# One transposing step and 512-column value products for each head of a differential attention

## The chip, the core and the metric

The kernel runs on one core of a Trainium2 chip. The metric is the time of one execution on the device in microseconds (us). Before the change it is 1768.67 us, the median of three runs (1768.25 to 1769.67). The engines are called PE (TensorE), DVE (VectorE), ACT (ScalarE), POOL (GpSimd) and SP (SyncE, which here issues most of the transfers).

## The reference, cut to what matters

The program is a trunk of two layers over 512 tokens of width 1024. Each layer computes three token mixers beside each other (a differential attention, a convolution module, a neighbourhood attention), merges them by gates, and adds a SwiGLU feed-forward part and a gated embedding. The change touches the differential attention alone. It has four heads in each layer, with two sets of queries and keys of width 64 and values of width 128:

```python
    def block(qi):
        s = jnp.einsum('bhcqd,bhckd->bhcqk', qi, k).astype(f32) * scale
        a = jax.nn.softmax(s, axis=-1)
        a = (a[:, :, 0] - lam * a[:, :, 1]).astype(v.dtype)
        return jnp.einsum('bhqk,bhkd->bhqd', a, v)

    o = lax.map(block, qb)
    o = o.transpose(1, 2, 0, 3, 4).reshape(B, HA, S, DV_A)
    o = rmsnorm(o, subln_g) * (1.0 - lam_init)
```

So for each head and each block of 128 queries there are two softmaxes over all 512 keys, their weighted difference, and the product with the values. The result is normalized over the value width.

## The kernel before

**Layout.** Activations lie with channels on the 128 partitions and the 512 tokens along the free axis. A matrix product of full precision is made of three products of a reduced format (`mm3`, lines 179 to 183): each operand is split in a high and a low part (`split`, lines 166 to 168: a copy on ACT gives the high part, a subtraction on DVE the low one), and high by high, high by low and low by high are accumulated. Weights are split the same way as they arrive (`weights`, lines 170 to 177, tiles named wr, wh and wl).

**Order of the work.** PE's instructions run in the order in which the program writes them. On the other engines a scheduler arranges the instructions when the kernel is built; in general the place in the program is the priority, and weight splits are put ahead. On the chip each engine then works through its list in order.

The long projections are written as loops of `mm3`. `chunk` (lines 119 to 122) counts these triples, and every fourth one is a tick (`tick`, lines 98 to 109), so a tick is 12 products of 512 columns. At each tick the small pieces of the attentions are put between the projection's products: first every running generator whose time has come makes its next step, then, where the gap since the last one has passed, the first unit in the queue is started. A `yield n` in such a generator means that it goes on n ticks later.

**A differential head.** `diff_in` (line 830) projects a head's queries and keys, applies the rotary embedding on DVE (tiles named rp; the halves are swapped by four transfers, line 846), splits the result and stacks high and low parts by transfers (`stack`, line 664). Then it queues four units, one for each block of 128 queries, at a gap of two ticks. Each unit calls `probs` (line 909): two score tiles of 128x512 in PSUM, four products; a maximum on DVE for each; two exponentials on ACT; and on DVE the difference of the two, which stays in a tile named a. The pool has three buffers of a, four of e (the second exponential) and two of b.

Every second unit goes on. Three ticks later it transposes the probabilities of its 256 queries on PE (line 876): eight transposes of 128x128 into two PSUM tiles (tag tr, two buffers), each of them for two of the four key blocks. Each PSUM tile is split into a tile pt of high and low parts. Two ticks later the products with the values follow: four key blocks, three products each, 256 columns wide, into one half of the accumulator av. After the second half the accumulator is squared and copied on ACT, and the norm over the value width runs with transposes one tick and three ticks later.

Between these pieces stand the projections of later heads, the value projections (`values`, products of 256 columns, line 619), and the gates (`gate_c`, `gate_b`). The taps of the convolution (tiles conv_z, line 164) are filled in on DVE as background work, behind chosen instructions.

Of the kernel before, what the change touches and what calls it, by code (L numbers as in the profile page):

```python
# [12 lines left out]
F32R = mybir.dt.float32r  # L13
# [7 lines left out]
P = 128  # L21
# [44 lines left out]
class Net:  # L66
# [794 lines left out]
    def diff_unit(self, head, qt, st4, k2, st, box, ys):  # L861

        nc, i = self.nc, self.i
        half, t = qt // 2, qt % 2
        box[qt] = self.probs(st4, k2, qt, box["s0"])
        if t == 0:
            return
        yield 3
        ats = [box[2 * half], box[2 * half + 1]]
        pps = []  # L870
        for kp in range(2):
            pt = self.ps("tr", (P, 2, 256))
            for u in range(2):
                for t in range(2):
                    kc = 2 * kp + u
                    nc.tensor.transpose(pt[:, u, t * P:(t + 1) * P],
                                        ats[t][:, kc * P:(kc + 1) * P], self.ident)
            pp = self.sb("pt", [P, 2, 2, 256], F32R)
            self.split(pp[:, 0], pp[:, 1], pt)
            pps.append(pp)  # L880
        yield 2
        if half == 0:
            box["av"] = self.ps("av")
        av = box["av"]
        cs = slice((head % 2) * P, (head % 2) * P + P)
        for kp in range(2):
            for u in range(2):
                v = st["v", head // 2][kp][:, u].rearrange("p (a b) -> p a b", a=2)
                self.mm3(av[:, half * 256:half * 256 + 256], v[:, 0, cs], v[:, 1, cs],
                         pps[kp][:, 0, u], pps[kp][:, 1, u], kp * 2 + u == 0, kp * 2 + u == 3)  # L890
        if half == 0:
            return

        eps = self.sb("sm", [P, 4])
        self.stt(eps, box["s0"], EPS, box["s0"], ALU.mult, ALU.mult)
        o = self.sb("t", [P, 512])
        sq = self.sb("ss", [P, 512])
        self.act(sq, av, AF.Square)
        self.act(o, av, AF.Copy, scale=self.subg[:, i:i + 1])

        def done(col, bc):
            self.tt(o, o, bc, ALU.mult)
            y = self.sb("y", [P, 2, 512], F32R)
            self.split(y[:, 0, :], y[:, 1, :], o)
            ys.append(y)

        yield from self.norm(sq, P, (1, 2), done, spread=False, eps=eps)

    def probs(self, st4, k2, qt, s0):


        nc, i = self.nc, self.i
        qs = slice(qt * P, (qt + 1) * P)
        m = self.sb("s", [P, 10])
        es = []
        for u in range(2):
            sc = self.ps("sc")
            self.scores(sc, st4, k2, u, qs, slice(0, 512))
            nc.vector.tensor_reduce(out=m[:, u:u + 1], in_=sc, op=ALU.max, axis=AX.X, negate=True)  # L919
            e = self.sb("e" if u else "a", [P, 512])  # L920
            self.act(e, sc, AF.Exp, table="exp", bias=m[:, u:u + 1],
                     accum_out=m[:, 3:4] if u else s0[:, qt:qt + 1])
            es.append(e)
        nc.vector.reciprocal(m[:, 4:5], m[:, 3:4])
        self.stt(m[:, 5:6], m[:, 4:5], self.nlam[:, i:i + 1], s0[:, qt:qt + 1],
                 ALU.mult, ALU.mult)
        self.stt(es[0], es[1], m[:, 5:6], es[0], ALU.mult, ALU.add)
        return es[0]
# [555 lines left out]
```

## Time and profile before

The profile is of one execution.

| what | before |
|---|---|
| median of the runs (lowest, highest) | 1768.67 us (1768.25, 1769.67) |
| span of the profiled execution | 1766.6 us |
| time from the span to the median | 2.1 us |
| PE busy | 1759.3 us, 100% |
| DVE busy | 1408.6 us, 80% |
| ACT busy | 885.5 us, 50% |
| POOL busy | 98.4 us, 6% |
| the chain that ended last | PE 92%, DVE 4%, DMA 2%, ACT 2% |

The span runs from the first to the last instruction of the program. The profiled execution's own time is its span and the little around it; the table sets the span beside the median of the runs. A row of the timeline has the start in us, the length in us, the engine, the line, the operation, the tile written and the tiles read, the shape, and how many such instructions follow each other; in brackets the idle time of the engine before it and what ended it. Matmuls overlap in PE's pipeline, so the length of one is more than the distance to the next.

### The profile page before, as it was taken

Reading aid. Unit: us, or ns where it says so; the run is one execution under the profiler, and the core shown is the slowest. Engines: PE = TensorE matmul, PEld = TensorE weight load, DVE = VectorE, ACT = ScalarE, POOL = GpSimd, SP = SyncE. Lnnn points to the kernel's source line nnn. Section 1 sums busy time; section 2 is a strip of 40 time slices with the busy share of each in tenths; the row PEclk is TensorE's granted clock in tenths of the full one; section 3 lists DMA queues with packets and bytes.
Section 4 is the critical chain, followed back from the end, with each engine's and each line's share of the span. In section 5 each row is a group of like instructions: output and inputs, shape, how many; then the busy total and the mean of one; then the engine's idle time right before and its main releaser. Section 6 shows DMA issues by size and latency. Waiting matters only on the chain.

```text
span 1766.6 us, 27127 instructions
## 1 busy us (share of the span) xinstructions
PE 1759.3 (100%) x10146; PEld 1551.8 (88%) x10146; DVE 1408.6 (80%) x2354; ACT 885.5 (50%) x1529; POOL 98.4 (6%) x114
## 2 busy tenths in 40 slices
PE   9999999999999999999999999999999999999998
PEld 7888888888899899998888888888888998989987
DVE  7967988998898587787777688889887976867776
ACT  5576555325565254454545655552356643534444
POOL 0000000000111010100000000000001110101000
PEclk9999999999999999999999999999999999999999
DMA  6575641334757365544446655322356674655332
GB/s 231 158 186 160 162 123 54 102 100 150 222 153 196 106 173 156 137 126 127 151 137 173 180 148 154 108 73 94 101 183 194 168 179 118 172 141 156 99 104 96
DMA packets 112548, 253.95 MB, mean 144 GB/s; under 512 B 14368, under 2 KB 23328, under 8 KB 112416
## 3 DMA queue, kind: packets, MB, share of 16 engines
q1 hardware_dynamic: 99024, 227.83, 42.0%
q0 software_dynamic: 12672, 23.07, 8.1%
q8 instruction: 80, 1.31, 0.3%
q10 hardware_dynamic: 720, 1.31, 0.2%
q14 instruction: 52, 0.43, 0.1%
HBM read 214.41 MB, written 7.34 MB: 126 GB/s over the span
## 4 chain that ended last, share of the span: by engine, by line
PE 92%; DVE 4%; DMA 2%; ACT 2%; issue 1%; SPq 0%; POOL 0%; ACTq 0%; POOLq 0%; DVEq 0%
PE ffn_mm L1034 4%; PE ffn_mm L1036 4%; PE ffn_mm L182 4%; PE ffn_mm L181 4%; PE ffn_mm L183 4%; PE ffn_mm L1035 4%; PE ffn_sc L1036 3%; PE ffn_sc L1034 3%; PE ffn_sc L1035 3%; PE mergea_mm L182 2%; PE mergea_mm L183 2%; PE mergea_mm L181 2%; PE gateb_mm L182 2%; PE gateb_mm L183 2%; PE gateb_mm L181 2%; PE wo_mm L182 2%
## 5 line engine op out<-in xcount | busy, mean ns | idle before, releaser
L164 DVE SCALAR_TENSOR_TENSOR conv_z<-glu_z,pre_par,conv_z 128x512 f32<-128x512 f32 x240 | 179.6, 748 | 3.5
L147 ACT ACTIVATE ffn_wh<-ffn_wr 128x1024 fp32r<-128x1024 f32 (+1 forms) x92 | 92.8, 1015 | 111.9 <-PE ffn_mm L182 81.4
L1004 POOL DMA_DIRECT2D ffn_qk<-w_fu x88 | 78.1, 978 | 605.6 <-DMA ffn_qk<-w_fu 289.7
L161 DVE TENSOR_TENSOR ffn_wl<-ffn_wr,ffn_wh 128x1024 fp32r<-128x1024 f32 (+1 forms) x92 | 107.4, 1173 | 5.3 <-ACT ffn_wh L147 4.6
L161 DVE TENSOR_TENSOR ffn_t<-ffn_mm,wo_rb 128x512 f32<-128x512 f32 (+1 forms) x64 | 38.7, 605 | 68.4 <-PE ffn_mm L183 68.4
L147 ACT ACTIVATE mergea_wh<-mergea_wr 128x1024 fp32r<-128x1024 f32 (+1 forms) x32 | 27.1, 848 | 96.8 <-PE mergea_mm L182 79.5
L147 ACT ACTIVATE ffn_wh<-ffn_qk 128x1024 fp32r<-128x1024 f32 x44 | 46.7, 1061 | 37.1 <-PE ffn_mm L182 15.9
L161 DVE TENSOR_TENSOR ffn_wl<-ffn_qk,ffn_wh 128x1024 fp32r<-128x1024 f32 x44 | 53.9, 1224 | 10.7 <-ACT ffn_wh L147 10.7
L161 DVE TENSOR_TENSOR ffn_t<-ffn_t,ffn_t 128x512 f32<-128x512 f32 (+1 forms) x46 | 31.3, 680 | 31.9 <-ACT ffn_t L147 31.4
L147 ACT ACTIVATE natten_e<-natten_e,natten_s 128x192 f32<-128x192 f32 (+1 forms) x88 | 39.3, 474 | 25.2 <-DVE natten_s L726 21.9
L181 PE MATMUL ffn_mm<-ffn_v,ffn_wh 128*128 128x512 f32 x132 | 51.4, 389 | 0.0
L182 PE MATMUL ffn_mm<-ffn_v,ffn_wh 128*128 128x512 f32 x132 | 51.4, 389 | 0.0
L183 PE MATMUL ffn_mm<-ffn_v,ffn_wl 128*128 128x512 f32 x132 | 51.3, 389 | 0.0
L181 PE MATMUL ffn_mm<-ffn_y,ffn_wh 128*128 128x512 f32 x132 | 51.3, 389 | 0.0
L182 PE MATMUL ffn_mm<-ffn_y,ffn_wh 128*128 128x512 f32 x132 | 51.3, 389 | 0.0
L183 PE MATMUL ffn_mm<-ffn_y,ffn_wl 128*128 128x512 f32 x132 | 51.3, 389 | 0.0
L147 ACT ACTIVATE diff_a<-diff_sc,diff_s 128x512 f32<-128x512 f32 x32 | 22.0, 687 | 57.1 <-DVE diff_s L919 57.0
L1036 PE MATMUL ffn_mm<-wo_h,ffn_wl 128*128 128x256 f32 x176 | 49.8, 283 | 0.0
L1036 PE MATMUL ffn_sc<-wo_h,ffn_wl 128*128 128x256 f32 x176 | 49.8, 283 | 0.0
L1035 PE MATMUL ffn_sc<-wo_h,ffn_wh 128*128 128x256 f32 x176 | 49.8, 283 | 0.0
L1035 PE MATMUL ffn_mm<-wo_h,ffn_wh 128*128 128x256 f32 x176 | 49.8, 283 | 0.0
L1034 PE MATMUL ffn_sc<-wo_h,ffn_wh 128*128 128x256 f32 x176 | 49.8, 283 | 0.0
(879 smaller groups left out, 6539.8 us busy)
## 6 DMA issues: line engine op xcount, KB each, us to landing
ffn_qk<-w_fu POOLq DMA_DIRECT2D x88, 256.0 KB, 5.7
ffn_wr<-w_fg SPq DMA_DIRECT2D x44, 512.0 KB, 3.7
ffn_wr<-w_fd SPq DMA_DIRECT2D x32, 448.0 KB, 4.1
ffn_r<-w_fu SPq DMA_DIRECT2D x44, 256.0 KB, 4.2
ffn_qk<-w_fg SPq DMA_DIRECT2D x44, 256.0 KB, 4.0
ffn_qk<-w_fu SPq DMA_DIRECT2D x44, 256.0 KB, 4.2
natten_wr<-w_in SPq DMA_DIRECT2D x16, 512.0 KB, 4.3
diff_wr<-w_in SPq DMA_DIRECT2D x16, 512.0 KB, 4.2
```

Of the source, the lines that this page charges most:

```text
L147: i = self.nc.scalar.activation(out, in_, func, **kw)
L161: return self.nc.vector.tensor_tensor(out, a, b, op)
L164: return self.nc.vector.scalar_tensor_tensor(out, a, s, b, op0, op1)
L181: mm(out, wh, ah, start=first, stop=False)
L182: mm(out, wh, al, start=False, stop=False)
L183: mm(out, wl, ah, start=False, stop=last)
L1004: nc.gpsimd.dma_start(q, wu[:, lo], accum_op=ALU.add)
L1034: mm(out, wh[:, c], bh, start=first and k == 0, stop=False, skip_group_check=True)
L1035: mm(out, wh[:, c], bl, start=False, stop=False, skip_group_check=True)
L1036: mm(out, wl[:, c], bh, start=False, stop=k == 3, skip_group_check=True)
```

## The change

The unit of a head no longer stops after every second block of queries. The first three units only make their probabilities. The fourth goes on for the whole head: three ticks later it transposes, for the first two key blocks, all 512 queries (two PSUM tiles of four transposes, one for each key block), splits them, and one tick later makes six products of 512 columns. Directly behind these it transposes for the other two key blocks, splits, and one tick later makes the other six products. The accumulator is taken when the first transposes are written, and no longer filled by halves.

Since all four tiles of probabilities now live until then, they take turns between the three buffers of a and the two of b, in the order a, b, a, b, a over the units of successive heads.

```diff
     def diff_unit(self, head, qt, st4, k2, st, box, ys):
 
         nc, i = self.nc, self.i
-        half, t = qt // 2, qt % 2
-        box[qt] = self.probs(st4, k2, qt, box["s0"])
-        if t == 0:
+        box[qt] = self.probs(st4, k2, qt, box["s0"], "ab"[(4 * head + qt) % 5 % 2])
+        if qt < 3:
             return
         yield 3
-        ats = [box[2 * half], box[2 * half + 1]]
-        pps = []
-        for kp in range(2):
-            pt = self.ps("tr", (P, 2, 256))
-            for u in range(2):
-                for t in range(2):
-                    kc = 2 * kp + u
-                    nc.tensor.transpose(pt[:, u, t * P:(t + 1) * P],
-                                        ats[t][:, kc * P:(kc + 1) * P], self.ident)
-            pp = self.sb("pt", [P, 2, 2, 256], F32R)
-            self.split(pp[:, 0], pp[:, 1], pt)
-            pps.append(pp)
-        yield 2
-        if half == 0:
-            box["av"] = self.ps("av")
-        av = box["av"]
+        av = self.ps("av")
         cs = slice((head % 2) * P, (head % 2) * P + P)
         for kp in range(2):
+            pps = []
+            for u in range(2):
+                kc = 2 * kp + u
+                pt = self.ps("tr", (P, 4, P))
+                for t in range(4):
+                    nc.tensor.transpose(pt[:, t], box[t][:, kc * P:(kc + 1) * P], self.ident)
+                pp = self.sb("pt", [P, 2, 512], F32R)
+                self.split(pp[:, 0], pp[:, 1], pt.rearrange("p a b -> p (a b)"))
+                pps.append(pp)
+            yield 1
             for u in range(2):
                 v = st["v", head // 2][kp][:, u].rearrange("p (a b) -> p a b", a=2)
-                self.mm3(av[:, half * 256:half * 256 + 256], v[:, 0, cs], v[:, 1, cs],
-                         pps[kp][:, 0, u], pps[kp][:, 1, u], kp * 2 + u == 0, kp * 2 + u == 3)
-        if half == 0:
-            return
+                self.mm3(av, v[:, 0, cs], v[:, 1, cs], pps[u][:, 0], pps[u][:, 1],
+                         kp + u == 0, kp + u == 2)
 
         eps = self.sb("sm", [P, 4])
...
-    def probs(self, st4, k2, qt, s0):
+    def probs(self, st4, k2, qt, s0, tag):
...
-            e = self.sb("e" if u else "a", [P, 512])
+            e = self.sb("e" if u else tag, [P, 512])
```

## The prediction

> **What bounds the kernel now.** I read the page first, then the waits of PE, then the timeline of PE around the differential heads, and last the timelines of DVE, ACT and SP beside it.
>
> ```profile
> span 1766.6 us, 27127 instructions
> PE 1759.3 (100%) x10146; PEld 1551.8 (88%) x10146; DVE 1408.6 (80%) x2354; ACT 885.5 (50%) x1529; POOL 98.4 (6%) x114
> ...
> DVE  7967988998898587787777688889887976867776
> ...
> PEclk9999999999999999999999999999999999999999
> ```
>
> The profiled execution spans 1766.6 us and PE is busy in all but 7 us of it, at a granted clock that never leaves the top digit. The median of the runs shown is 1768.67 us, 2.1 us above that span, so I work out a difference on the profile and add it to the median. The DVE row matters next: in slices five to seven (44 us each, so 177 to 309 us, where layer 0's differential heads run) it stands at 9, 8, 8.
>
> ```profile
> engine line waited for: us in total, times, longest us
> PE pre_av L329 <- DVE pre_zeror L402: 1.1, 1, 1.1
> PE natten_av L763 <- DVE natten_a L161: 0.3, 1, 0.3
> ```
>
> That is the whole list of what PE waited for: 1.4 us in the execution. So the end is set by PE's own stream, which is written out by hand. Whatever takes products out of it, or makes it wait, moves the end by the same amount; whatever happens on another engine costs nothing until PE waits for it. The second list entry is small, but the first has nothing to do with the change either: PE never waits for the differential heads' splits today.
>
> ```profile
> L181 PE MATMUL diff_av<-diff_pt,diff_v x64: 277/283/283, 193.0 to 1176.2; 128*128 128x256 f32 x64
> ...
> L147 ACT ACTIVATE diff_pt<-diff_tr x32: 573/587/602, 187.3 to 1170.0; 128x512 fp32r<-128x512 f32 x32
> L161 DVE TENSOR_TENSOR diff_pt<-diff_tr,diff_pt x32: 680/683/692, 189.9 to 1170.9; 128x512 fp32r<-128x512 f32 x32
> ```
>
> These groups count the step that is changed: lines 181 to 183 have 64 products of 256 columns each (the other two lines show the same count), 192 in all, 24 for each of the eight heads; 32 copies on ACT at 587 ns and 32 subtractions on DVE at 683 ns, four and four for each head.
>
> **What a product costs on PE.** A row's duration holds the pipeline's depth, so the price is the distance between starts. The next fence is PE's timeline in layer 0's head 0.
>
> ```profile
> 182.99 0.39 PE L181 MATMUL diff_mm<-glu_h,diff_wh 128*128 128x512 f32 x1
> ...
> 185.71 1.03 PE L876 MATMUL diff_tr<-pre_ident,diff_a 128*128 128x128 f32 x8
> 186.50 0.47 PE L181 MATMUL diff_mm<-glu_h,diff_wh 128*128 128x512 f32 x1
> ...
> 192.98 0.28 PE L181 MATMUL diff_av<-diff_pt,diff_v 128*128 128x256 f32 x1
> ...
> 194.41 0.28 PE L619 MATMUL diff_mm<-diff_wh,glu_h 128*128 128x256 f32 x1
> ...
> 201.09 1.04 PE L876 MATMUL diff_tr<-pre_ident,diff_a 128*128 128x128 f32 x8
> 201.88 0.36 PE L619 MATMUL diff_mm<-diff_wh,glu_h 128*128 128x256 f32 x1
> ...
> 204.84 0.40 PE L828 MATMUL diff_sc<-diff_qk 128*128 128x512 f32 x1
> ...
> 205.76 0.28 PE L619 MATMUL diff_mm<-diff_wh,glu_h 128*128 128x256 f32 x1
> ...
> 208.63 0.28 PE L181 MATMUL diff_av<-diff_pt,diff_v 128*128 128x256 f32 x1
> ```
>
> From 182.99 to 185.71 lie 12 projection products of 512 columns: 2.72 us, 227 ns each. From 192.98 to 194.41 lie the 12 products of a half head, 256 columns: 1.43 us, 119 ns each. Eight transposes take 186.50 - 185.71 = 0.79 us, four scores 205.76 - 204.84 = 0.92 us, and a tick's products here (24 of 256 columns) behind transposes 204.84 - 201.88 = 2.96 us.
>
> **Removed and added.** A head gives up 24 products of 256 columns (2 x 1.43 = 2.86 us) and gets 12 of 512 columns (2.72 us). Gain 0.14 us a head, times eight: 1.1 us, all of it on the path. Both rows fit a constant of some 12 ns per product beside 0.42 ns per column (227 = 12 + 512 x 0.42, 119 = 12 + 256 x 0.42), and it is twelve such constants a head that go. The Trainium skill, "TensorE: Matmul & The Clock Gate", section "Back-to-back issue gap", gives 2.5 ns beside N/2.4 instead; by that the gain would be 12 x 8 x 2.5 = 0.24 us, so trace and page differ, and I keep the trace's.
>
> The transposes stay 16 a head in two groups of eight, the ACT copies and DVE subtractions stay four and four of 128x512, so the count of work on PE's, ACT's and DVE's queues doesn't change otherwise. No DMA is issued in the step, so nothing of it passes SP or POOL. Five buffers (three "a", two "b") serve four tiles of one head and the first of the next; the next head's second unit needs the buffer of this head's first, but its scores stand on PE behind the second group of transposes that frees it, so its exponential can't be held up by that. I cost the tags at nothing; if a bias tile still held a "b", one exponential would slip, and its reader is three ticks away.
>
> **Moved.** Call a head's first unit's tick T. Before: transposes of half 0 at T+5 and products at T+7, of half 1 at T+9 and T+11. After: all at the end, transposes of the first key pair at T+9, their products and the second pair's transposes at T+10, the second products at T+11. The head ends at the same tick, so the norm and what reads the head move only by what PE gains or loses. But the time from a transpose to the product that reads it shrinks from two ticks to one. In the fence above it was 208.63 - 201.09 = 7.54 us.
>
> With one tick, the first pair's first product comes 0.79 + 2.96 = 3.75 us after its transposes begin, needs the first subtraction one product later (3.98 us) and the second four products later (4.66 us). The second pair has the scores of the next head's unit in its tick: 0.79 + 0.92 + 2.96 = 4.67 us, with needs at 4.9 and 5.6 us. A product that waits holds up everything behind it on PE: transposes, scores, projections. So the question is how late DVE ends the subtractions. An ordinary head shows this:
>
> ```profile
> 232.50 1.03 PE L876 MATMUL diff_tr<-pre_ident,diff_a 128*128 128x128 f32 x8
> 233.28 0.48 PE L181 MATMUL gatec_mm<-glu_h,gatec_wh 128*128 128x512 f32 x1
> ...
> 236.10 0.39 PE L828 MATMUL diff_sc<-diff_qk 128*128 128x512 f32 x1
> ...
> 233.47 1.07 ACT L147 ACTIVATE diff_pt<-diff_tr 128x512 fp32r<-128x512 f32 x2
> ...
> 233.60 1.23 DVE L161 TENSOR_TENSOR gatec_wl<-gatec_wr,gatec_wh 128x1024 fp32r<-128x1024 f32 x1
> 234.74 1.28 DVE L161 TENSOR_TENSOR diff_pt<-diff_tr,diff_pt 128x512 fp32r<-128x512 f32 x2
> ```
>
> Head 1's transposes begin at 232.50; the copies end at 234.54 (2.0 us later), DVE finishes a weight subtraction, and both tile subtractions end at 236.02, 3.5 us later. Here the tick has 512-column products: 236.10 - 233.28 = 2.82 us, so the first product would come at 3.6 us and the second subtraction is needed at 4.5 us. There is 1 us to spare, more in the second pair. I cost heads 1 to 3 at nothing; the cover is that tick, and without the margin each further weight subtraction (1.23 us) ahead would cost about 0.2 us of waiting.
>
> Head 0 is different, because the rotary work of a later head lies there:
>
> ```profile
> 202.31 1.06 ACT L147 ACTIVATE diff_pt<-diff_tr 128x512 fp32r<-128x512 f32 x2
> ...
> 201.28 0.68 DVE L161 TENSOR_TENSOR diff_rp<-diff_rp,diff_r 128x512 f32<-128x512 f32 x1
> ...
> 202.55 1.22 DVE L161 TENSOR_TENSOR diff_wl<-diff_wr,diff_wh 128x1024 fp32r<-128x1024 f32 x1
> 203.68 0.69 DVE L161 TENSOR_TENSOR diff_rp<-diff_rp,diff_r 128x512 f32<-128x512 f32 x1
> 204.28 0.69 DVE L161 TENSOR_TENSOR diff_pt<-diff_tr,diff_pt 128x512 fp32r<-128x512 f32 x1
> 204.89 0.68 DVE L161 TENSOR_TENSOR diff_rp<-diff_rp,diff_rp 128x512 f32<-128x512 f32 x1
> ...
> 207.15 0.69 DVE L161 TENSOR_TENSOR diff_rp<-diff_rp,diff_r 128x512 f32<-128x512 f32 x1
> 207.75 0.68 DVE L161 TENSOR_TENSOR diff_pt<-diff_tr,diff_pt 128x512 fp32r<-128x512 f32 x1
> 208.35 0.68 DVE L161 TENSOR_TENSOR diff_rp<-diff_rp,diff_rp 128x512 f32<-128x512 f32 x1
> ```
>
> The copies end at 203.37, 2.3 us after the transposes began at 201.09. The first subtraction ends at 204.97 (3.9 us), but then DVE does five other things, rotary steps and a tap, and the second ends only at 208.44: 7.35 us. Today PE asks for it at 208.63 or later. The same in layer 1:
>
> ```profile
> 1076.11 1.03 PE L876 MATMUL diff_tr<-pre_ident,diff_a 128*128 128x128 f32 x8
> ...
> 1079.52 0.69 DVE L161 TENSOR_TENSOR diff_pt<-diff_tr,diff_pt 128x512 fp32r<-128x512 f32 x1
> ...
> 1082.98 0.69 DVE L161 TENSOR_TENSOR diff_pt<-diff_tr,diff_pt 128x512 fp32r<-128x512 f32 x1
> ```
>
> There the ends lie 4.1 and 7.56 us after 1076.11. If this order stayed, PE would wait 7.35 - 4.66 = 2.7 us in layer 0 and 7.56 - 4.66 = 2.9 us in layer 1, 5.6 us in all.
>
> It won't simply stay. The T+5 and T+7 work (0.79 + 1.43 = 2.2 us) is gone from PE ahead of T+9, so these transposes begin at about 198.9, while the rotary steps hang on transfers that SP issues in its own order:
>
> ```profile
> 194.50 2.45 SPq L846 DMA_DIRECT2D diff_rp<-diff_rp  x4
> ...
> 197.68 2.41 SPq L846 DMA_DIRECT2D diff_rp<-diff_rp  x4
> ```
>
> Those issues (four pieces each) end at 196.95 and 200.09; the first rotary product ran at 201.28. SP was busy with the previous head's stacking before, which hardly moves. So the first pair's copies would end at about 201.2, just as the rotary work begins: the subtractions have nothing or one to two older instructions (0.6 to 1.2 us) ahead, and end between 202.5 and 204.5, against needs at 198.9 + 3.98 = 202.9 and 203.6. That is a wait of 0 to 0.9 us. The second pair's transposes begin at about 204.0 (198.9 + 3.75 + six products of 0.227), their copies end at 206.3, and the rotary steps, which ended at 209.03 before, are pushed back by two subtractions; if all of them go first the second pair ends at about 210, against a need at 204.0 + 5.6 = 209.6: 0 to 0.5 us. I take 1.0 us a layer for head 0, between the ends 0 and 2.9, nearer to the lower because the shift by 2.2 us is sure and the order is not.
>
> Sum: -1.1 + 2 x 1.0 = +0.9 us, on the profile 1767.5, on the median 1769.6 us.
>
> **The rivals.** *No wait at all.* DVE takes the two subtractions in head 0 before the rotary work. For: the 2.2 us, and PE's list is empty of such waits today. Against: one tick is less than half of the former distance. Then -1.1 us: 1767.6 us.
>
> *Slower: the second subtraction stays behind the rotary steps.* Place: head 0 of each layer, PE's fifth product of the first pair. Its price is the 5.6 us above, plus up to 0.5 us a layer where the second pair is late too: -1.1 + 5.6 = +4.5, 1773.2 us, at most 1774.2. It decides from the point where more than two rotary steps stand between the two subtractions. For it speaks that both layers show exactly this order now, and that queues are set in order of the program, in which the rotary work of a later head stands ahead of these transposes. Against it speaks the shift.
>
> *A wait that brings the clock down.* The clock row has no digit below 9, and no wait over 1.1 us, so nothing here shows what a wait of 2.9 us does. The Trainium skill's same page, section "Why this matters for your kernels", warns of PE-idle gaps over about 3 us, after which the rate halves; no run here shows it. At half rate, a stretch of products as long as the 5.6 us of waits would cost as much again: 1773.2 + 5.6 = 1778.8 us.
>
> *Faster beyond what can be told.* A measurement of this kernel can tell about 0.2%, 3.5 us, from no change. The gain of 1.1 us and all of PE's 1.4 us of waits together don't reach it; only a reshuffle of the queues far from here could, for which I see no row.
>
> **How the numbers follow.** Forecast (a wait of part of the time, net -0.5 to +3.5 us) 0.38; no wait 0.22; second subtraction behind the rotary steps 0.32; clock or lateness in all heads (above 1774) 0.04; faster by over 0.2% 0.04. So within 0.2%: 0.60, slower 0.36. The range runs from 1767.2, just under the case without waits, to 1774.2, the slower rival with both pairs late; it leaves out some 0.08 at the ends and about as much in what I haven't thought of. The forecast's own range is 1768.2 to 1772.2.
>
> **What would show it.** In the changed kernel's PE timeline 12 products of 512 columns a head at 227 ns, transposes at 198.9 and 204.0 in head 0. In PE's waits a new entry: products of lines 181 or 182 into the accumulator waiting for DVE's subtraction, in head 0 of each layer, about 1 us each; none in heads 1 to 3. On DVE, at most two instructions between the two subtractions of head 0's first pair. The prediction is wrong if PE's new waits sum to over 4.6 us, if they lie in the ordinary heads, if 512-column products here cost more than 230 ns, or if the end moves without a new wait on PE.

## The result, and the profile after

The changed kernel takes 1774.79 us (median of five runs, 1774.13 to 1777.24) where the kernel before takes 1769.43 us in the same comparison. The ratio is 1.0036, with a 95% interval of 1.0024 to 1.0048: 5.4 us, or 0.36%, slower. The profiled execution is the longest of the five, 1777.24 us with a span of 1775.1 us.

The page of the changed kernel, the lines that answer to those of before:

```profile
span 1775.1 us, 26929 instructions
PE 1762.0 (99%) x10050; PEld 1548.0 (87%) x10050; DVE 1409.4 (79%) x2354; ACT 885.2 (50%) x1529; POOL 98.2 (6%) x114
...
PEclk9999999999999999999999999999999999999999
```

PE's instructions are 96 fewer, as the change says (12 products less in each of eight heads), and yet the span is 8.5 us longer. The waits of PE say where most of it went (in each row: who waited for whom, us in total, times, the longest):

```profile
PE diff_av L182 <- DVE diff_pt L161: 4.9, 6, 1.4
PE pre_av L329 <- DVE pre_zeror L402: 1.1, 1, 1.1
PE diff_mm L181 <- DVE natten_y L161: 1.0, 1, 1.0
...
```

The first row is new: the value products of line 182, the first that need a low part, wait for DVE's subtraction, six times. The third, a projection behind the neighbourhood part, is not in the profile of before either and comes up again below. PE's timeline of layer 0 shows the places of the first row:

```profile
200.80 0.27 PE L876 MATMUL diff_tr<-pre_ident,diff_a 128*128 128x128 f32 x1
...
204.54 0.40 PE L181 MATMUL diff_av<-diff_pt,diff_v 128*128 128x512 f32 x1
...
205.24 0.40 PE L181 MATMUL diff_av<-diff_pt,diff_v 128*128 128x512 f32 x1
206.48 0.50 PE L182 MATMUL diff_av<-diff_pt,diff_v 128*128 128x512 f32 x1 [0.85 <-DVE diff_pt L161]
206.82 0.40 PE L183 MATMUL diff_av<-diff_pt,diff_v 128*128 128x512 f32 x1
...
233.13 0.38 PE L876 MATMUL diff_tr<-pre_ident,diff_a 128*128 128x128 f32 x2
...
236.74 0.39 PE L181 MATMUL diff_av<-diff_pt,diff_v 128*128 128x512 f32 x1
238.45 0.50 PE L182 MATMUL diff_av<-diff_pt,diff_v 128*128 128x512 f32 x1 [1.32 <-DVE diff_pt L161]
...
239.02 0.40 PE L181 MATMUL diff_av<-diff_pt,diff_v 128*128 128x512 f32 x1
239.65 0.50 PE L182 MATMUL diff_av<-diff_pt,diff_v 128*128 128x512 f32 x1 [0.23 <-DVE diff_pt L161]
```

In head 0 the transposes begin at 200.80 and the first product comes 3.74 us later, as forecast. The fifth product starts at 206.48, 1.24 us behind the fourth, where 0.227 us is the rule: 1.0 us of waiting. In head 1 the second product starts 1.71 us behind the first and the fifth 0.63 us behind the fourth: 1.5 and 0.4 us. Layer 1 has the same three (1.0, 1.5, 0.4 us), so the six waits make 5.8 us by the distances (the list counts only the time in which PE stands idle, 4.9 us).

### The profile page after: what moved, and what is told of

Its sections match the earlier page's. It is cut to its first block, busy times and chain, and to the rows that moved or that the text cites. A ratio compares the mean times of both kernels' runs of the same rounds, so it can differ in the third digit from the quotient of the medians.

```text
span 1775.1 us, 26929 instructions
## 1 busy us (share of the span) xinstructions
PE 1762.0 (99%) x10050; PEld 1548.0 (87%) x10050; DVE 1409.4 (79%) x2354; ACT 885.2 (50%) x1529; POOL 98.2 (6%) x114
## 4 chain that ended last, share of the span: by engine, by line
PE 88%; DVE 5%; ACT 2%; DMA 2%; issue 1%; SPq 0%; POOL 0%; DVEq 0%; ACTq 0%; POOLq 0%
PE ffn_mm L1026 4%; PE ffn_mm L1028 4%; PE ffn_mm L181 4%; PE ffn_mm L182 4%; PE ffn_mm L183 4%; PE ffn_mm L1027 4%; PE ffn_sc L1028 3%; PE ffn_sc L1026 3%; PE ffn_sc L1027 3%; PE mergea_mm L181 2%; PE mergea_mm L183 2%; PE mergea_mm L182 2%; PE gateb_mm L181 2%; PE gateb_mm L182 2%; PE wo_mm L181 2%; PE gateb_mm L183 2%
## 5 line engine op out<-in xcount | busy, mean ns | idle before, releaser
L1027 PE MATMUL ffn_mm<-wo_h,ffn_wh 128*128 128x256 f32 x176 | 49.8, 283 | 0.0
L1026 PE MATMUL ffn_mm<-wo_h,ffn_wh 128*128 128x256 f32 x176 | 49.8, 283 | 0.0
```

Source lines behind the costliest of these rows:

```text
L1026: mm(out, wh[:, c], bh, start=first and k == 0, stop=False, skip_group_check=True)
L1027: mm(out, wh[:, c], bl, start=False, stop=False, skip_group_check=True)
```

## Experiments

The theory after the result: in heads 0 and 1 rotary steps stand ahead of the tile subtractions in DVE's order, and with one tick between transposes and products PE meets them. The rivals: one tick is too short in any order; the wide products or the regrouped transposes cost PE more; the shared buffers hold up exponentials; and, for part of the time, waits bring the clock down. DVE's timeline of the changed kernel, head 0 first, then head 1:

```profile
203.28 0.69 DVE L161 TENSOR_TENSOR diff_pt<-diff_tr,diff_pt 128x512 fp32r<-128x512 f32 x1
203.88 0.68 DVE L161 TENSOR_TENSOR diff_rp<-diff_rp,diff_r 128x512 f32<-128x512 f32 x1
204.48 0.74 DVE L164 SCALAR_TENSOR_TENSOR conv_z<-glu_z,pre_par,conv_z 128x512 f32<-128x512 f32 x1
205.15 0.68 DVE L161 TENSOR_TENSOR diff_rp<-diff_rp,diff_r 128x512 f32<-128x512 f32 x1
205.75 0.68 DVE L161 TENSOR_TENSOR diff_pt<-diff_tr,diff_pt 128x512 fp32r<-128x512 f32 x1
```

```profile
235.84 0.69 DVE L161 TENSOR_TENSOR diff_rp<-diff_rp,diff_r 128x512 f32<-128x512 f32 x1
236.44 0.75 DVE L164 SCALAR_TENSOR_TENSOR conv_z<-glu_z,pre_par,conv_z 128x512 f32<-128x512 f32 x1
237.10 0.69 DVE L161 TENSOR_TENSOR diff_rp<-diff_rp,diff_r 128x512 f32<-128x512 f32 x1
237.71 0.69 DVE L161 TENSOR_TENSOR diff_pt<-diff_tr,diff_pt 128x512 fp32r<-128x512 f32 x1
238.31 0.68 DVE L161 TENSOR_TENSOR diff_rp<-diff_rp,diff_rp 128x512 f32<-128x512 f32 x1
238.91 0.68 DVE L161 TENSOR_TENSOR diff_pt<-diff_tr,diff_pt 128x512 fp32r<-128x512 f32 x1
```

In head 0 three instructions stand between the two subtractions: a rotary step, a tap, a rotary step. In head 1 the first subtraction comes behind two rotary steps and a tap, and another rotary step stands before the second; it ends at 239.59, 6.5 us after the transposes began at 233.13. The copies on ACT that these two subtractions read had long ended, at 235.47:

```profile
234.40 1.07 ACT L147 ACTIVATE diff_pt<-diff_tr 128x512 fp32r<-128x512 f32 x2
```

**The changed kernel once more** (no edit).

> The changed kernel once more, as the one to compare with on the same chip. If the waits sit in a fixed order of DVE's work, the same six waits of PE for the tile subtractions come back: about 1.0 us in head 0 and 1.5 + 0.4 us in head 1 of each layer, 5.8 us in all, and the ratio to the kernel before is 1.003 to 1.004. If the stretch of half clock (3.4 us from 1117.9 us in the first profile) follows from those waits, one or two such stretches of 3.4 us come again, in head 1 of a layer; if it was an accident, none. The 1.1 us wait of a projection at 157 us behind the neighbourhood part came with late rotary transfers and should be gone or elsewhere.

Measured: 1775.81 us against 1769.07, ratio 1.0038 (1.0025 to 1.0051).

```profile
PE diff_av L182 <- DVE diff_pt L161: 4.9, 6, 1.4
...
PE diff_mm L181 <- DVE natten_y L161: 0.9, 1, 0.9
```

The same six waits came back, at the same places and of the same length. No stretch of half clock is in this profile. The projection's wait came again, this time in layer 1. It does not belong to the change: it is in eight of the fourteen profiles, 0.3 to 1.0 us each time, one of them that of the kernel in the old halves with one tick (0.7 us).

**Splits put ahead.**

```diff
-                self.split(pp[:, 0], pp[:, 1], pt.rearrange("p a b -> p (a b)"))
+                with self.tc.high_priority(offset=min(HIGH, self.tc.cur_priority - self.p0)):
+                    self.split(pp[:, 0], pp[:, 1], pt.rearrange("p a b -> p (a b)"))
```

> The splits of the transposed probabilities get a higher place in the scheduler's order, so that on ACT and DVE they stand ahead of the rotary steps; PE's order and the one tick stay. Theory (the wait comes from the rotary steps standing ahead of the second subtraction): the waits of the value products fall from 5.8 us to under 0.5 us, the clock stays at the top, and the time is that of before less the 1.1 us of the twelve products saved a head: ratio to before 0.999 to 1.000. Rival (one tick is too short for copies and subtractions whatever their order): over 3 us of waits remain, ratio 1.002 or more. Second rival (wide products or the regrouped transposes cost PE more): no waits, but ratio still 1.002 or more.

Measured: 1768.65 us, ratio to before 0.9996 (0.9988 to 1.0005). The waits of PE and DVE's order in head 1:

```profile
PE pre_av L329 <- DVE pre_zeror L402: 1.1, 1, 1.1
PE natten_av L763 <- DVE natten_a L161: 0.3, 1, 0.3
PE diff_sc L828 <- DMA diff_x<-diff_rp: 0.2, 1, 0.2
```

```profile
232.22 1.22 DVE L161 TENSOR_TENSOR gatec_wl<-gatec_wr,gatec_wh 128x1024 fp32r<-128x1024 f32 x1
233.36 1.28 DVE L161 TENSOR_TENSOR diff_pt<-diff_tr,diff_pt 128x512 fp32r<-128x512 f32 x2
234.56 0.68 DVE L161 TENSOR_TENSOR diff_rp<-diff_rp,diff_r 128x512 f32<-128x512 f32 x1
```

No value product waits any more. DVE does both subtractions directly behind the weight subtraction and the rotary step follows. The edit raises the splits' copies on ACT too, and in all heads; one tick, wide products, tags and PE's order are as in the changed kernel. So one tick is enough in this order, and neither the wide products nor the regrouping cost anything that the trace or the time shows. The order of the splits against the rotary steps is the cause, and since the copies had ended before DVE came to the subtractions, it is DVE's order that counts.

**The same, in head 0 alone and in head 1 alone** (the offset is HIGH in that head and 0 in the others).

> The changed kernel with the splits put ahead in head 0 alone. If the waits add up head by head, head 0's (2 x 1.0 us) vanish and head 1's stay (2 x 1.9 us): waits of the value products 3.8 us, time 1772 to 1774 us. If one late spot feeds the next (the rotary steps that are pushed back in head 0 come later in head 1), head 1's waits change too.

> The changed kernel with the splits put ahead in head 1 alone: head 0's waits of 1.0 us a layer stay (2.0 us), head 1's vanish; 1770.5 to 1772 us. Together with the run of head 0 alone the two gains should add up to what both bring, some 6 to 7 us.

Measured: head 0 alone 1774.01 us, ratio 1.0030 (1.0018 to 1.0041); head 1 alone 1770.96 us, 1.0012 (1.0003 to 1.0021). The first row here is that of head 0 alone, the second that of head 1 alone:

```profile
PE diff_av L182 <- DVE diff_pt L161: 4.5, 4, 1.4
```

```profile
PE diff_av L182 <- DVE diff_pt L161: 1.7, 2, 0.8
```

Against 1775.81 us, head 0 brings 1.8 us and head 1 4.85 us, 6.65 together, where both bring 7.16 (1775.81 - 1768.65). These are medians of separate comparisons, with intervals of some 2 us either way; within that the two add up, and head 1 is the larger part. With head 0 alone, head 1's waits grow a little (1.07 instead of 0.4 us at its fifth product): in this list a tap (at 236.97 us) stands between head 1's two subtractions beside the rotary step. So the spots do feed each other somewhat, through the list, and its time lies at the upper edge of what was expected.

**Without the rotary steps.**

```diff
-            self.act(raw, ps, AF.Copy, scale=1.0 if s else 0.125)
+            self.background(self.act(raw, ps, AF.Copy, scale=1.0 if s else 0.125), self.bg["diff"])
...
-            self.background(self.tt(raw, raw, st["tabs"][0], ALU.mult), self.bg["diff"])
-            self.tt(rot, rot, st["tabs"][1], ALU.mult)
-            self.tt(raw, raw, rot, ALU.add)
```

> The changed kernel without the rotary embedding's three DVE steps for the differential queries and keys (they are used as projected; the transfers that swap the halves are still issued, and their tiles are not read). No priorities are changed. If the rotary steps are what stands ahead of the late subtractions, PE's waits for DVE's subtractions fall from 4.9 us to under 1 us. If DVE is late for another reason (weight subtractions, taps), over 3 us stay.

Measured: one run of 1765.66 us, span 1763.7 us. All waits of PE in it:

```profile
PE pre_av L329 <- DVE pre_zeror L402: 1.1, 1, 1.1
PE natten_av L763 <- DVE natten_a L161: 0.3, 1, 0.3
```

Without a change of priorities the waits for subtractions are gone. What stood ahead of the late subtractions was the rotary work, with the taps that hang on its first step. Those taps hang on ACT's copy here, so this run takes both out of the way and does not tell their shares. The span is 2.9 us below that of the kernel before: 1.1 us are the products, and where the other 1.8 us come from was not followed up.

**Two ticks for the first pair.**

```diff
-            yield 1
+            yield 2 - kp
```

> The first pair of key blocks gets two ticks between transposes and products, the second keeps one; a head ends one tick later. Theory (too short a distance in front of the rotary steps): no waits at the first pair, clock at the top, ratio 0.999 to 1.000. Rival (buffers): the first tile of probabilities is now held until behind the next head's second scores, so that head's exponential waits for it about a tick, and PE waits for scores or probabilities instead, ratio 1.002 or more.

Measured: 1769.22 us, ratio 1.0000 (0.9991 to 1.0009).

```profile
PE diff_av L182 <- DVE diff_pt L161: 0.5, 1, 0.5
```

The first pair, which got the second tick, waits nowhere, as expected, though rotary steps still stand ahead of its subtractions and between them: a longer distance covers that order. Two small waits are left in layer 1, both at the second pair, which kept one tick (0.3 and 0.7 us by the distances). No scores or probabilities wait: the buffer rival is out, though the first tile is held longer here.

**The tags alone, in the kernel before** (the probabilities' tiles take turns in a and b as in the change, all else as before).

> The kernel before with the probabilities' tiles in turn in the buffers of a and b, all else as before. Theory (the tags cost nothing): no wait of PE that the kernel before doesn't have, ratio 1.000. Rival (the shared buffers hold up an exponential): new waits of PE for scores or probabilities, ratio over 1.001.

Measured: 1769.19 us, ratio 1.0000 (0.9991 to 1.0009), and PE's waits are the two of before. The tags cost nothing.

**One tick in the kernel before.**

```diff
             pps.append(pp)
-        yield 2
+        yield 1
```

> The kernel before with one tick instead of two between the transposes of a half head and its products; halves, widths and tags stay as before. Theory (the distance against DVE's order): the products of head 0 wait for the subtractions in each layer, 1 to 3 us a layer, perhaps those of head 1 too; ratio to before 1.001 to 1.004. Rival (the cost is in the wide products, the regrouping or the place at the head's end): no waits, ratio 1.000.

Measured: 1792.0 us, ratio 1.0125 (1.0111 to 1.0139), far above what was expected.

```profile
PE diff_av L182 <- DVE diff_pt L161: 8.4, 8, 1.8
PE diff_tr L876 <- DVE diff_t L161: 6.7, 6, 2.0
```

The first row is the mechanism that was expected: 8.4 us, all in head 0 of both layers. The second row was not: transposes wait for the norm. PE's timeline of one such place:

```profile
256.69 0.60 PE L231 MATMUL diff_tr<-pre_ident,diff_rc 128*128 128x128 f32 x4
257.12 0.60 PE L876 MATMUL diff_tr<-pre_ident,diff_a 128*128 128x128 f32 x4
259.74 0.66 PE L876 MATMUL diff_tr<-pre_ident,diff_a 128*128 128x128 f32 x4 [2.02 <-DVE diff_t L161]
```

One tick less for the second half also brings the norm's broadcast (line 231) one tick forward, into the tick of the next head's transposes (line 876). Four of these find a free PSUM tile; the next four need the tile that the norm's multiplication on DVE still reads, and PE waits 2.0 us. So this run shows that distance alone makes waits in the old halves too, but its size belongs to two causes, and three stretches of half clock are in its profile besides (from 194.6, 1099.1 and 1146.9 us).

**Products in place of the waits.**

```diff
             yield 1
+            if kp == 0 and head < 2:
+                for _ in range((5, 9)[head]):
+                    nc.tensor.matmul(av, self.zero_r, self.zero_r[:, None, :].to_broadcast([P, 4, P]),
+                                     start=True, stop=True)
```

> The changed kernel with products of zeros put ahead of the first pair's value products, five of 512 columns in head 0 and nine in head 1 of each layer (5 x 0.227 = 1.1 us and 2.0 us): PE works where it waited for 1.0 and 1.9 us. If waiting brings the clock down, no stretch of half clock is left, the waits are under 0.3 us, and the time is that of the changed kernel + 2 x (3.1 - 2.9) - 1.7 to 3.4 us, so 1 to 3 us below it, with nearly no spread among the runs. If the clock falls for another reason, the stretches stay and the time is 0.5 us above the changed kernel.

Measured: 1775.77 us, ratio 1.0035 (1.0022 to 1.0047).

```profile
PE diff_mm L181 <- DVE natten_y L161: 1.9, 2, 1.0
```

Beside this there is only a score's wait of 0.2 us for a transfer that the kernel before does not have. The value products wait no more and there is no stretch of half clock in the profile, but the time equals that of the changed kernel (1775.81 us); neither forecast came true, since the first had it 1 to 3 us below and the second 0.5 us above with the stretches still there. The 6.3 us of filling took the place of 5.8 us of waits and the 0.7 us behind them that the next run brings up; the profiled execution also had two late projections, 2.2 us by the distances. So in the typical execution the waits cost little more than their length, and this run does not settle what part the clock has.

**No tick at all before the second pair's products.**

```diff
-            yield 1
+            if kp == 0:
+                yield 1
```

> The changed kernel without the tick between the second pair's transposes and their products: PE must wait there in every head, about 2.3 us in head 0 and 0.9 us in the others (the second subtraction ended 4.0 and 2.6 us after the transposes began, the six products need 2.15 us), 5 us a layer, 10 us in all beside the 5.8 us of before: 1783 to 1787 us. If waiting brings the clock down, there are several stretches of half clock in the profile, 1.7 us each on top; if the stretch in the first profile was an accident, none.

Measured: 1789.79 us, ratio 1.0118 (1.0103 to 1.0134).

```profile
PE diff_av L182 <- DVE diff_pt L161: 10.0, 18, 1.5
PE diff_av L181 <- ACT diff_pt L147: 2.2, 8, 0.3
```

All heads wait now, 12.2 us in 26 places by the list, and the time is 3 us above what was expected. Part of that is that each wait costs more than itself: the product behind it is followed at 0.34 us and not at 0.227 (in the changed kernel 206.48 to 206.82), 0.11 us that I had not counted, some 2 us over the 18 places of line 182. One stretch of half clock is in the profile (from 209.8 us), directly behind head 0's waits, and none in layer 1 behind waits at the same places.

**Products of 256 columns in the kernel with the splits ahead** (each of the 12 made as two).

> The kernel with the splits put ahead, with each product of 512 columns made as two of 256: 24 products a head again, all else the same. By the trace's distances (119 and 227 ns) it is 1.1 us slower than the kernel with the splits ahead: 1769.8 us where that has 1768.65. By a constant of 2.5 ns a product it is 0.24 us slower, which can't be told. The trace should give 24 x 0.120 = 2.87 us a head against 2.72 us.

Measured: 1769.60 us, ratio to before 1.0002 (0.9993 to 1.0011), 0.95 us above the run with wide products in another comparison, which these intervals can't tell from zero. The trace can. Half a head, first with wide products, then with narrow ones:

```profile
240.13 0.39 PE L181 MATMUL diff_av<-diff_pt,diff_v 128*128 128x512 f32 x1
...
241.49 0.39 PE L181 MATMUL gatec_mm<-glu_h,gatec_wh 128*128 128x512 f32 x1
```

```profile
241.92 1.60 PE L887 MATMUL diff_av<-diff_pt,diff_v 128*128 128x256 f32 x12
243.35 0.40 PE L181 MATMUL gatec_mm<-glu_h,gatec_wh 128*128 128x512 f32 x1
```

Six wide products take 1.36 us, twelve narrow ones 1.43 us. That is 0.07 us a half head, 1.1 us over the kernel.

**The kernel with the splits ahead, once more.**

> The kernel with all the splits put ahead, once more, because its first comparison with the kernel before (0.9996) left the sign open. By the twelve constants saved a head it should be 1.1 us faster, ratio 0.9994, an interval of some 0.1% either way, so even two comparisons may leave it open; in the profile no wait of PE for a subtraction and no stretch of half clock.

Measured: 1768.33 us, ratio 0.9997 (0.9988 to 1.0006). This is the best version: 6.5 to 7.2 us below the changed kernel. Against the kernel before, two comparisons of eleven runs each put it 0.4 and 0.6 us ahead, and both intervals hold 1; that it is faster fits the sum and is not shown.

## Why the prediction was right or wrong

**What bounds the kernel** was right: PE's stream sets the end, and nothing costs until PE waits.

**The products' gain**, 1.1 us, was right by the distances (1.36 against 1.43 us); the times alone do not show it. The Trainium skill, "TensorE: Matmul & The Clock Gate", section "Back-to-back issue gap", gives a constant of 2.5 ns a product in what it calls the isolated gap, which by estimate would make it 0.24 us; these products, 227 and 119 ns apart, do not fit it.

**Head 0**, 1.0 us a layer, was right in place and size: the fifth product of the first pair, 1.0 us in both layers. That the size came out so well is in part luck: 1.0 us was picked between 0 and 2.9, and three instructions stand between the two subtractions (203.97 to 205.75 us) where I had said one or two would be ahead. The transposes began at 200.80 us and not at 198.9; 1.1 us of that is the late projection (in the run with two ticks, where no projection is late in layer 0, they begin at 198.95). The second pair waited nowhere; its 0 to 0.5 us fell on the lower end.

**Heads 1 to 3 at nothing** is the step that failed. Head 1 costs 1.9 us a layer, twice head 0; heads 2 and 3 do cost nothing. I read in the trace of before that both subtractions ended 3.5 us after the transposes, and took that row over to the changed kernel. But the rotary step that came right behind those subtractions (in the changed kernel at 235.84) was near enough to pass them: it stands ahead of them in the new list. For head 0 I had argued that the order would be made anew; for head 1 I treated the same list as fixed, and called 1 us to spare a cover. The sum with head 1's measured waits is -1.1 + 2.0 + 3.8 = +4.7 us, and with the 0.7 us behind six waits +5.4 us, against 5.4 us measured (late projections and the clock left out). Two of the signs that I had named for being wrong came: the new waits sum to 5.8 us, over 4.6, and the larger part lies in head 1. The rival that ends slower was right in its mechanism, rotary steps ahead of the subtractions. Its point of decision, more than two rotary steps between the two subtractions, was not reached: there are two and a tap in head 0, whose price was 1.0 and not 2.7 to 2.9 us a layer, and one in head 1. It reached nearly the measured time (1773.2 us) with the wrong head.

**The clock rival**, which I gave hardly any chance, shows in the profiled execution. The page's row PEclk can't show it: 3.4 us at half clock leave a slice of 44 us in the top digit. First the granted clock in two stretches of layer 1, then PE around the first:

```profile
1117.90:1121.30 3.40, 3.40 (x13) 2.95 (x12) 3.02 (x6) 1.19 (x2) 0.00 (x0) 0.50 0.80 186
1121.30:1124.70 3.40, 3.40 (x16) 2.78 (x15) 1.78 (x5) 2.31 (x5) 0.00 (x0) 1.00 0.54 125
```

```profile
1115.92 0.50 PE L182 MATMUL diff_av<-diff_pt,diff_v 128*128 128x512 f32 x1 [1.37 <-DVE diff_pt L161]
...
1117.12 0.50 PE L182 MATMUL diff_av<-diff_pt,diff_v 128*128 128x512 f32 x1 [0.24 <-DVE diff_pt L161]
...
1119.62 0.63 PE L828 MATMUL diff_sc<-diff_x,diff_qk 128*128 128x512 f32 x1
1120.05 0.63 PE L828 MATMUL diff_sc<-diff_qk 128*128 128x512 f32 x1
```

From 1117.9 us on, behind head 1's two waits, PE runs at half its rate for 3.4 us, with scores 0.43 us apart where 0.227 is usual: 1.7 us. With that, the waits and the late projection explain the profiled span: -1.1 + 5.8 + 1.7 + 1.1 = 7.5 us, and 6 x 0.11 = 0.7 us behind the waits, make 8.2 of the 8.5 us. The Trainium skill, "TensorE: Matmul & The Clock Gate", section "What's actually happening", gives a free-running window of 3413 ns over which activity decides; the length agrees. The Trainium skill's same page, section "Why this matters for your kernels", warns of gaps over about 3 us; here the longest single idle time was 1.37 us, so the measurement goes further than that warning.

How often this happens is open. Such stretches are in one of the two profiles of the changed kernel, in those with one tick in the old halves (three) and with no tick (one), always within a few us behind waits; none is in the other ten (all fourteen are at half clock at the very end, where PE has no work left). The mean clock of each execution, profiled or not, points the same way: it is 0.998 or less in all eight of the kernels with one tick in the old halves and with no tick, in two of the changed kernel's ten, in two of six with head 0 alone put ahead, and in none of 65 of the kernel before that were run beside the experiments. But one execution of the kernel with the splits ahead also shows a mean clock of 0.998 and 2.8 us more than its median, so waits in these heads are not shown to be the only way to it.

**The range** ended at 1774.2 us, at the slower rival with head 0 alone; head 1's waits together with head 0's put the median 0.6 us beyond it.

## What to carry to other kernels

When a wait is given less room, do not read the new slack from the old trace's order: the scheduler makes the list anew, and every older instruction that is ready near the spot can pass the one that PE needs. List for each shortened wait what work of earlier priority becomes ready within the old distance, and put the operation that the bounding engine needs ahead of it, which here took one line and brought back about 7 us. A regrouping that saves instructions on a full engine is worth only their constants (12 ns each here), so the 1.1 us of all eight heads together are gone with one new wait of 1 us.

## What the runs showed of the hardware that was not expected

A product of 512 columns that has waited is followed by the next after 0.34 us (206.48 to 206.82 us), not 0.227 us, so six waits cost 0.7 us beside their length. With 256 columns, in the kernel before with one tick, it is 0.22 to 0.23 us where 0.119 us is the rule.

The clock fell to half for 3.4 us behind waits of 1.37 and 0.24 us of idle time, and in the other profiled execution of the same kernel it did not behind the same waits.

Transfers land at times that differ by over 1 us from one execution to the next. In the changed kernel's profile DVE waits for the rotary transfer of a later head, before the first changed instruction:

```profile
151.75 0.69 DVE L161 TENSOR_TENSOR diff_rp<-diff_rp,diff_r 128x512 f32<-128x512 f32 x1 [2.31 <-DMA diff_rp<-diff_rp]
```

In the kernel before it started this step at 150.18 us after 0.69 us of idle time, and in the second profile of the same changed kernel at 150.61 us after 0.87 us. In the first execution this lateness ends as the projection's wait of 1.0 us in layer 0; in the second the projection waits in layer 1 (0.9 us).
